# Small products of the two mixers issued in another order: level by level across four quarters of the TensorE array instead of block by block in one

## The chip, the core and the metric

The kernel runs on one core of one Trainium2 chip. The metric is the device time of one execution in microseconds (us). TensorE (PE in the profile) multiplies 128 rows by 128 columns; a product whose operands are smaller can be put on a part of the array with `tile_position=(row, column)`, and here the parts are tiles of 32x32, 128 rows x 32 columns, or 64x64. VectorE (DVE), ScalarE (ACT) and GpSimd (POOL) do the elementwise work, SyncE (SP) issues the loads of the weights.

## What is computed

One transformer layer over 256 tokens of width 2048 in float32. The normed input goes through one projection, which feeds eight heads of gated DeltaNet (GDN) and eight heads of HGRN2; the outputs of both groups go through one output projection with a residual, and a squared-ReLU feed-forward of width 8192 follows, with a residual and a last norm. Cut to what matters:

```python
def gated_delta_rule_chunked(q, k, v, beta, g):
    unit_lower = jnp.where(strict, beta[..., :, None] * kk * decay, 0.0) + jnp.eye(CHUNK, dtype=jnp.float32)
    sol = lax.linalg.triangular_solve(unit_lower, rhs, left_side=True, lower=True, unit_diagonal=True)
    ...
def hgrn2_chunked(q, k, v, log_f):
    # S_t = diag(f_t) S_{t-1} + k_t v_t^T (k_t = 1 - f_t),  o_t = S_t^T q_t
    a_diag = jnp.einsum('bhsid,bhsijd,bhsjd->bhsij', qc, d_diag, kc)
    ...
def hybrid_token_mixer(n, w_in, ...):
    proj = n @ w_in
    ...
    y = jnp.concatenate([y_a, y_b], axis=-1).astype(n.dtype)
    return y @ w_out
...
    h = h + hybrid_token_mixer(...)
    h = h + jnp.square(jax.nn.relu(rms_norm(h) @ w_ff1)) @ w_ff2
return rms_norm(h)
```

## The kernel before

**The projections.** Every weight tile is split into a high part `hi` (ACT, L117) and a rest `lo` (DVE, L118), and TensorE multiplies both: L281 (512 columns) with `hi`, L282 (256 columns) with `lo`. The result of two feature tiles is gathered in two `acc` tiles, then ACT copies (L288) and DVE adds and scales (L289, L290). The same split feeds the output projection (L655) and the feed-forward (L700, L701, L717).

**The mixers.** The kernel goes through 16 heads, and the projection of the next head stands beside the mixer of the one before it. The heads 0 to 7 are GDN; their lower triangular systems, two of 128 rows for each head, are gathered and solved together. `gdn_invert` inverts the 32x32 blocks on POOL (L413 to L427, some 60 us in a row), and `gdn_solve` (L430 to L504, called once, at the second HGRN2 head) puts the inverse together on TensorE: `Xn` holds the inverted 32x32 blocks of the 16 systems (`NB`), four of each. For the two halves `u` = 0 (rows 0 to 63) and 1 (rows 64 to 127) it multiplies the lower left block of each system with `Xn` (L454, into `pP`, the tile (0, 32) or (64, 96)), ACT negates it into `Pn` (L456), a second product goes into the other rows of `pP` (L458, the tile (32, 0) or (96, 64)), and DVE copies that into `Y` (L460). Then come `pX` (L462), two rounds of 64x64 products `pp` (L470, L475), and the products with V (L483 on). The other eight heads are HGRN2, in `hgrn_mix` (L512 to L610); they are called head 0 to 7 below. DVE prepares `E`, the keys and queries with the decays of six levels (L561, L562); TensorE then makes 40 small products into `pd`: for each of 8 blocks of 32 tokens four products of 32 columns (L575) and one of 64 (L578), on the column quarter 32q of the array, with q the number of the block modulo 4. Behind them stand three more products into `pa` (L583, L587, L589). DVE and POOL add `pd` up into `A` (L592 to L599), ACT copies `pa` to it, and `A` is multiplied with V into `poh` (L608, L609). A norm over the head follows in `finish_heads` (its products are `pm`, L393 and L394, from `shi` and `slo`, L391 and L392).

**The order.** The functions are written one after the other, but a planner takes all the instructions, with modelled durations, and writes one fixed order for each engine; each engine works its row off in that order and waits where an operand isn't there. PSUM holds four `acc` tiles, two tiles for `hgrn_mix` (`mx`) and two for the solve (`sv`), so the planner's order also depends on when these come free. All the work of the solve stands somewhere among the projections of the heads 2 to 5.

Of the kernel before, what the change touches and what calls it, by code (L numbers as in the profile page):

```python
# [16 lines left out]
T = 256  # L17
# [7 lines left out]
NL = len(LEVELS)  # L25
NM = NL + 1
# [47 lines left out]
def hybrid_block(ctx: ExitStack, tc: tile.TileContext, x, xt, w_in, w_ab, params, w_out, w_ff1, w_ff2,  # L74
                 norm_final_w, consts, out):
    nc = tc.nc
    PE, ACT, DVE, POOL, SP = nc.tensor, nc.scalar, nc.vector, nc.gpsimd, nc.sync

    def view(ap, off, dims):
        return bass.AP(ap.tensor, ap.offset + off, [list(ap.ap[0])] + [list(d) for d in dims])  # L80
# [24 lines left out]
    def mx(name):  # L105
        return psM.tile([P, 512], F32, tag="mx", name=name)
# [297 lines left out]
    NB = 2 * NH  # L404
# [25 lines left out]
    def gdn_solve(Xn):  # L430
# [13 lines left out]
        def amat(i, rows, c):  # L444
            hd, t = divmod(i, 2)
            return PA(hd)[rows, 1, t * T + c.start:t * T + c.stop]

        pP, pX = sv("pP"), sv("pX")
        Pn = Xn
        for u in range(2):  # L450
            lo_, hi_ = 64 * u, 64 * u + 32
            L_, H_ = slice(lo_, lo_ + 32), slice(hi_, hi_ + 32)
            for i in range(NB):
                PE.matmul(pP[H_, 32 * i:32 * i + 32], lhsT=amat(i, L_, H_), rhs=Xn[L_, i, :],  # L454
                          start=True, stop=True, tile_position=(lo_, hi_))
            ACT.activation(Pn[H_].rearrange("p a m -> p (a m)"), pP[H_, :], AF.Copy, scale=-1.0)  # L456
            for i in range(NB):
                PE.matmul(pP[L_, 32 * i:32 * i + 32], lhsT=Pn[H_, i, :], rhs=Yd[H_, i, :],  # L458
                          start=True, stop=True, tile_position=(hi_, lo_))
            DVE.tensor_copy(Y[L_, :, H_], pP[L_, :].rearrange("p (a m) -> p a m", m=32))  # L460
        for i in range(NB):
            PE.matmul(pX[32:64, 32 * i:32 * i + 32], lhsT=Yd[32:64, i, :], rhs=Pn[32:64, i, :],  # L462
                      start=True, stop=True, tile_position=(32, 32))
        ACT.copy(X6[32:64, :, 0:32], pX[32:64, :].rearrange("p (a m) -> p a m", m=32))
        for half in range(2):
            pp = sv("pp")
            hs = slice(8 * half, 8 * half + 8)
            for n in range(8):
                i = 8 * half + n
                PE.matmul(pp[64:128, 64 * n:64 * n + 64], lhsT=amat(i, slice(0, 64), slice(64, 128)), rhs=X6[:, i, :],  # L470
                          start=True, stop=True, tile_position=(0, 64))
            ACT.activation(P6[64:128, hs].rearrange("p a m -> p (a m)"), pp[64:128, :], AF.Copy, scale=-1.0)
            for n in range(8):
                i = 8 * half + n
                PE.matmul(pp[0:64, 64 * n:64 * n + 64], lhsT=P6[64:128, i, :], rhs=Y[64:128, i, 64:128],  # L475
                          start=True, stop=True, tile_position=(64, 0))
# [19 lines left out]
        for pair in range(NH // 2):  # L496
            po = sv("po")
            for n in range(2):
                hd, c = 2 * pair + n, n * T
# [11 lines left out]
    def hgrn_mix(hd, R):  # L511
# [6 lines left out]
        u = mp.tile([P, 4, T], F32, tag="u", name="u", bufs=UB)  # L518
# [6 lines left out]
        gx = mp.tile([P, 4, T], F32, tag="gx", name="gx")  # L525
        KQ, pb = gx[:, 0:2], gx[:, 2:4]
# [16 lines left out]
        E = mp.tile([P, NL + 2, T], F32, tag="big", name="E")  # L543
# [23 lines left out]
                          op=ALU.mult)  # L567

        pd, pa = mx("pd"), mx("pa")
        for blk in range(8):  # L570
            t, q = divmod(blk, 4)
            s = slice(32 * blk, 32 * blk + 32)
            c = t * NM * 32
            for n in range(1, NL):
                PE.matmul(pd[32 * q:32 * q + 32, c:c + 32], lhsT=E[:, n, s], rhs=E[:, n, s], start=True, stop=True,  # L575
                          tile_position=(0, 32 * q))
                c += 32
            PE.matmul(pd[32 * q:32 * q + 32, c:c + 64], lhsT=KQ[:, 0, s], rhs=view(gx, T + 32 * blk, [[T, 2], [1, 32]]),  # L578
                      start=True, stop=True, tile_position=(0, 32 * q))
        for c in range(4):  # L580
            t, q = divmod(c, 2)
            o0 = t * T + 64 * q + 32
            PE.matmul(pa[64 * q:64 * q + 32, o0:o0 + 32], lhsT=E[:, 0, 64 * c:64 * c + 32],  # L583
                      rhs=E[:, 0, 64 * c + 32:64 * c + 64], start=True, stop=True, tile_position=(0, 64 * q))
        for t in range(2):
            o0 = t * T + 64
            PE.matmul(pa[0:64, o0:o0 + 64], lhsT=E[:, NL, t * P:t * P + 64],  # L587
                      rhs=E[:, NL + 1, t * P + 64:t * P + 128], start=True, stop=True)
        PE.matmul(pa[:, P:T], lhsT=L[:, 0].rearrange("p a t -> p (a t)"), rhs=L[:, 1].rearrange("p a t -> p (a t)"),  # L589
                  start=True, stop=True)  # L590
# [24 lines left out]
    for n in range(2 * NH):  # L615
        if n + 1 < 2 * NH:
            nx = gdn_project(n + 1) if n + 1 < NH else hgrn_project(n + 1 - NH)
        if n == SOLVE_AT:
            gdn_solve(Xn)
        if n < NH:  # L620
            gdn_mix(n, *st)
        else:
            hgrn_mix(n - NH, st)
        if n == INVERT_AT:
            Xn = gdn_invert()
        st = nx
# [16 lines left out]
    for nh in range(2):  # L643
        accs = [acc_a() for _ in range(4)]
        for kp in range(8):
            w = wtile()
            SP.dma_start(w, w_out[nh * 8 + kp])
            for kk in range(2):
                k = 2 * kp + kk
                hi, lo = split(w[:, kk * 1024:(kk + 1) * 1024], 1024)  # L650
                for hf in range(2):
                    for a, ww in ((0, hi), (T, hi), (0, lo)):
                        st = yT(k, a + hf * P, a + hf * P + P)
                        for c in range(2):
                            PE.matmul(accs[2 * hf + c], lhsT=st, rhs=ww[:, c * 512:(c + 1) * 512],  # L655
                                      start=(k == 0 and a == 0 and ww is hi), stop=(k == 2 * NH - 1 and ww is lo))
# [64 lines left out]
    for f in range(NF):  # L721
# [4 lines left out]
        n = f - (NF - TAIL)  # L726
# [20 lines left out]
    for hf in range(2):  # L747
# [13 lines left out]
        s = fin[:, 2 * NP + hf:2 * NP + hf + 1]  # L761
# [61 lines left out]
```

## Times and profile before

| | us |
|---|---|
| median of three runs | 1284.4 (1284.13 to 1284.76) |
| the profiled execution, its own time | 1285.84 |
| its span (first to last instruction on the engines) | 1283.9 |
| TensorE busy in the span | 1252.5 (98%) |
| VectorE busy | 858.5 (67%) |
| ScalarE busy | 673.8 (52%) |
| GpSimd busy | 180.4 (14%) |

The time beside the span is 1.94 us. Busy time is the time in which an engine works on at least one instruction. The stages on the span's clock: the GDN heads to about 250 us, POOL's inversion from 259 to 322, the HGRN2 heads with the solve from 264 to 509, the output projection from 457 on between them, and the feed-forward from 570 to the end. The rows further down give times on the same clock.

### The profile page before, as it was taken

What the parts mean: (1) busy time and instruction counts of PE and PEld (TensorE: products, weight loads), DVE (VectorE), ACT (ScalarE), POOL (GpSimd) and SP (SyncE); (2) the same over time, 40 slices, a digit from 0 to 9 for tenths busy, and PEclk for the clock granted to TensorE, in tenths of its full rate; (3) what the DMA queues carried; (4) which work ended last, traced back from release to release, by engine and by line L of the source; (5) the groups of instructions that cost most, each with busy time, mean ns of one, the idle gap of its engine ahead of it and who ended that gap; (6) DMA issues with size and microseconds to landing.
All of it is one profiled execution on the core that took longest, in us unless ns stands there. A gap on an engine that the chain in (4) does not pass through costs nothing.

```text
span 1283.9 us, 18498 instructions
## 1 busy us (share of the span) xinstructions
PE 1252.5 (98%) x7290; PEld 1063.2 (83%) x7290; DVE 858.5 (67%) x1200; ACT 673.8 (52%) x972; POOL 180.4 (14%) x224
## 2 busy tenths in 40 slices
PE   6999999998899999999999999999999999999997
PEld 5888888877788887888888888888888888888885
DVE  8789999888867996565556555565555555555556
ACT  7567677655556874454444443444444444444453
POOL 4233433278301121000000000000000000000000
PEclk9999999998999999999999999999999999999999
DMA  7455555543423644455555555555555555555552
GB/s 289 166 160 184 174 180 192 171 140 131 149 100 131 217 151 168 154 203 191 194 173 190 196 174 189 197 175 186 197 195 190 188 191 192 194 194 197 197 200 95
DMA packets 34646, 229.65 MB, mean 179 GB/s; under 512 B 4408, under 2 KB 5184, under 8 KB 7808
## 3 DMA queue, kind: packets, MB, share of 16 engines
q1 hardware_dynamic: 32256, 225.32, 49.8%
q0 software_dynamic: 1728, 2.11, 1.3%
q8 instruction: 57, 0.93, 0.3%
q10 hardware_dynamic: 576, 1.05, 0.2%
q14 instruction: 29, 0.24, 0.1%
HBM read 225.83 MB, written 2.63 MB: 178 GB/s over the span
## 4 chain that ended last, share of the span: by engine, by line
PE 91%; DVE 3%; POOL 3%; issue 2%; DMA 1%; ACT 0%; SPq 0%; POOLq 0%; DVEq 0%; ACTq 0%
PE acc L281 15%; PE acc L717 14%; PE accb L717 13%; PE accb L700 9%; PE acc L700 9%; PE acc L282 8%; PE acc L655 7%; PE accb L701 5%; PE acc L701 5%; POOL Xt L419 1%; POOL X L421 1%; PE pd L575 1%; DVE xT L163 1%; DMA big<-in_xt_dram 1%; PE pk L363 1%
## 5 line engine op out<-in xcount | busy, mean ns | idle before, releaser
L118 DVE TENSOR_TENSOR lo<-w,hi 128x1024 fp32r<-128x1024 f32 x408 | 511.5, 1255 | 364.6 <-ACT hi L117 364.1
L117 ACT CAST hi<-w 128x1024 fp32r<-128x1024 f32 (+1 forms) x416 | 432.6, 1042 | 447.3 <-PE accb L717 177.2
L281 PE MATMUL acc<-xT,hi 128*128 128x512 f32 x1024 | 363.2, 401 | 9.6 <-ACT hi L117 8.5
L282 PE MATMUL acc<-xT,lo 128*128 128x256 f32 x1024 | 282.8, 285 | 4.8 <-DVE lo L118 4.7
L281 PEld LDWEIGHTS acc<-xT,hi 128*128 128x128 f32 x1024 | 191.0, 190 | 49.1 <-ACT hi L117 8.5
L282 PEld LDWEIGHTS acc<-xT,lo 128*128 128x128 f32 x1024 | 194.8, 191 | 12.1 <-DVE lo L118 6.2
L700 PE MATMUL acc<-hT,hi 128*128 128x512 f32 x512 | 181.3, 399 | 0.0
L700 PE MATMUL accb<-hT,hi 128*128 128x512 f32 x512 | 180.8, 398 | 0.0
L717 PE MATMUL accb<-hi,gs 128*128 128x512 f32 x496 | 170.6, 389 | 0.0
L701 PE MATMUL accb<-hT,lo 128*128 128x256 f32 x512 | 143.2, 281 | 0.0
L701 PE MATMUL acc<-hT,lo 128*128 128x256 f32 x512 | 142.8, 281 | 0.0
L717 PE MATMUL acc<-hi,gs 128*128 128x512 f32 x496 | 133.4, 389 | 0.0
L700 PEld LDWEIGHTS accb<-hT,hi 128*128 128x128 f32 x512 | 96.1, 188 | 23.9
L700 PEld LDWEIGHTS acc<-hT,hi 128*128 128x128 f32 x512 | 96.1, 188 | 23.4
L159 POOL TENSOR_TENSOR fin<-fin,cst 128x1 f32<-128x1 f32 x2 | 1.1, 566 | 777.0 <-PE accb L717 769.5
L717 PEld LDWEIGHTS acc<-hi,gs 128*128 128x128 f32 x496 | 93.0, 188 | 19.4
L717 PEld LDWEIGHTS accb<-hi,gs 128*128 128x128 f32 x496 | 93.1, 188 | 19.3
L701 PEld LDWEIGHTS acc<-hT,lo 128*128 128x128 f32 x512 | 96.5, 189 | 0.2
L701 PEld LDWEIGHTS accb<-hT,lo 128*128 128x128 f32 x512 | 96.6, 189 | 0.1
L717 PE MATMUL accb<-lo,gs 128*128 128x512 f32 x248 | 95.8, 389 | 0.0
L717 PE MATMUL acc<-lo,gs 128*128 128x512 f32 x248 | 77.2, 389 | 0.0
L717 PEld LDWEIGHTS acc<-lo,gs 128*128 128x128 f32 x248 | 46.6, 188 | 9.7
(248 smaller groups left out, 1323.6 us busy)
## 6 DMA issues: line engine op xcount, KB each, us to landing
w<-in_w_ff_dram SPq DMA_DIRECT2D x128, 1024.0 KB, 4.9
w<-in_w_in_dram SPq DMA_DIRECT2D x62, 1024.0 KB, 5.0
w<-in_w_out_dram SPq DMA_DIRECT2D x16, 1024.0 KB, 4.9
big<-in_xt_dram SPq DMA_DIRECT2D x4, 512.0 KB, 7.9
w<-in_w_in_dram SPq DMA_DIRECT2D x4, 512.0 KB, 8.1
h<-in_x_dram SPq DMA_DIRECT2D x2, 1024.0 KB, 9.2
dt<-scr_g POOLq DMA_DIRECT2D x8, 128.0 KB, 5.6
nfw<-in_norm_final_w_dram SPq DMA_DIRECT2D x1, 1024.0 KB, 4.7
```

The costliest lines, as they stand in the source:

```text
L117: ACT.copy(hi, w)
L118: eng.tensor_tensor(out=lo, in0=w, in1=hi.bitcast(F32), op=ALU.subtract)
L163: DVE.scalar_tensor_tensor(out=dst[:, k, T:2 * T], in0=pt, scalar=wcol, in1=dst[:, k, 0:T].bitcast(F32), op0=ALU.mult, op1=ALU.subtract)
L281: PE.matmul(accs[g], lhsT=hi[:, kk, g, :], rhs=xT[:, k, :], start=(k == 0), stop=False)
L282: PE.matmul(accs[g][:, T:], lhsT=lo[:, kk, g, :], rhs=xT[:, k, 0:T], start=False, stop=(k == KT - 1))
L363: PE.matmul(pk0, lhsT=R[:, 1, 0:P], rhs=qk.rearrange("p a t -> p (a t)"), start=True, stop=True)
L419: POOL.tensor_tensor(out=t3, in0=X[:, j, j + 1:].unsqueeze(2).to_broadcast([np_, nr, ncol]), in1=X[:, j, 0:ncol].unsqueeze(1).to_broadcast ...
L421: POOL.tensor_tensor(out=X[:, j + 1:, 0:ncol], in0=X[:, j + 1:, 0:ncol], in1=t3, op=ALU.subtract)
L655: PE.matmul(accs[2 * hf + c], lhsT=st, rhs=ww[:, c * 512:(c + 1) * 512], start=(k == 0 and a == 0 and ww is hi), stop=(k == 2 * NH - 1 and ...
L700: PE.matmul(accs[f], lhsT=hi[:, cs], rhs=hT[:, k, :], start=(k == 0), stop=False)
L701: PE.matmul(accs[f][:, T:], lhsT=lo[:, cs], rhs=hT[:, k, 0:T], start=False, stop=(k == KT - 1))
L717: PE.matmul(accs[hf][c], lhsT=gs[:, a + hf * P:a + hf * P + P], rhs=ww[:, cs], start=(f == 0 and a == 0 and ww is hi), stop=(f == NF - 1 a ...
```

## The change

Two groups of loops are written in another order; no product, copy or operand is added or taken away. In `gdn_solve` the two halves `u` stand inside the loop over the 16 systems, so that the products of both halves alternate; the two copies of ACT and the two of DVE follow behind each group. In `hgrn_mix` the loop over the levels stands outside and that over the 8 blocks inside, so that a product stands on another quarter than its neighbours.

```diff
 def gdn_solve(Xn):
-        for u in range(2):
-            lo_, hi_ = 64 * u, 64 * u + 32
-            L_, H_ = slice(lo_, lo_ + 32), slice(hi_, hi_ + 32)
-            for i in range(NB):
+        LH = [(64 * u, 64 * u + 32, slice(64 * u, 64 * u + 32), slice(64 * u + 32, 64 * u + 64)) for u in range(2)]
+        for i in range(NB):
+            for lo_, hi_, L_, H_ in LH:
                 PE.matmul(pP[H_, 32 * i:32 * i + 32], lhsT=amat(i, L_, H_), rhs=Xn[L_, i, :],
                           start=True, stop=True, tile_position=(lo_, hi_))
+        for lo_, hi_, L_, H_ in LH:
             ACT.activation(Pn[H_].rearrange("p a m -> p (a m)"), pP[H_, :], AF.Copy, scale=-1.0)
-            for i in range(NB):
+        for i in range(NB):
+            for lo_, hi_, L_, H_ in LH:
                 PE.matmul(pP[L_, 32 * i:32 * i + 32], lhsT=Pn[H_, i, :], rhs=Yd[H_, i, :],
                           start=True, stop=True, tile_position=(hi_, lo_))
+        for lo_, hi_, L_, H_ in LH:
             DVE.tensor_copy(Y[L_, :, H_], pP[L_, :].rearrange("p (a m) -> p a m", m=32))
...
 def hgrn_mix(hd, R):
-        for blk in range(8):
-            t, q = divmod(blk, 4)
-            s = slice(32 * blk, 32 * blk + 32)
-            c = t * NM * 32
-            for n in range(1, NL):
-                PE.matmul(pd[32 * q:32 * q + 32, c:c + 32], lhsT=E[:, n, s], rhs=E[:, n, s], start=True, stop=True,
-                          tile_position=(0, 32 * q))
-                c += 32
-            PE.matmul(pd[32 * q:32 * q + 32, c:c + 64], lhsT=KQ[:, 0, s], rhs=view(gx, T + 32 * blk, [[T, 2], [1, 32]]),
-                      start=True, stop=True, tile_position=(0, 32 * q))
+        for n in range(1, NL + 1):
+            for blk in range(8):
+                t, q = divmod(blk, 4)
+                s = slice(32 * blk, 32 * blk + 32)
+                c = t * NM * 32 + (n - 1) * 32
+                if n < NL:
+                    PE.matmul(pd[32 * q:32 * q + 32, c:c + 32], lhsT=E[:, n, s], rhs=E[:, n, s], start=True, stop=True,
+                              tile_position=(0, 32 * q))
+                else:
+                    PE.matmul(pd[32 * q:32 * q + 32, c:c + 64], lhsT=KQ[:, 0, s],
+                              rhs=view(gx, T + 32 * blk, [[T, 2], [1, 32]]),
+                              start=True, stop=True, tile_position=(0, 32 * q))
```

In the changed file some lines have other numbers: L454 is L453 there, L458 L459, L462 L464, L470 L472, L475 L477, L575 L578, L578 L581, L583 L587, L587 L591, L589 L593, L592 L596.

The planner is run anew on the changed program. The row of TensorE at the first HGRN2 head, before (the dots stand for seven more pairs of L575 and L578):

```order
L282 MATMUL acc<-xT,lo 128x256
L575 MATMUL pd<-E 32x32 x4
L578 MATMUL pd<-gx 32x64
...
L583 MATMUL pa<-E 32x32 x4
L587 MATMUL pa<-E 64x64 x2
L589 MATMUL pa<-L 128x128
```

The same place in the changed kernel:

```order
L282 MATMUL acc<-xT,lo 128x256
L578 MATMUL pd<-E 32x32 x32
L581 MATMUL pd<-gx 32x64 x8
L587 MATMUL pa<-E 32x32 x4
L591 MATMUL pa<-E 64x64 x2
L593 MATMUL pa<-L 128x128
```

The products are the same 40; the 32 short ones now stand in front of the 8 long ones, and two neighbours are never in one quarter.

TensorE at the first product of the solve, which stands inside the `pd` of head 2; before, with the half u = 0 alone (the numbers behind the names tell the tiles apart):

```order
L282 MATMUL acc_3623<-xT_100,lo_3647 128x256
L575 MATMUL pd_3544<-E_3522 32x32 x3
L454 MATMUL pP_2945<-Xn_2427,big_83 32x32 x10
L454 MATMUL pP_2945<-Xn_2427,PA1_141 32x32 x6
L575 MATMUL pd_3544<-E_3522 32x32
L578 MATMUL pd_3544<-gx_3511 32x64
```

In the changed kernel, where one of the 32 products of both halves is inside that `pd` and 31 stand behind seven products of the projection:

```order
L578 MATMUL pd_3544<-E_3522 32x32 x4
L453 MATMUL pP_2945<-Xn_2427,big_83 32x32
L578 MATMUL pd_3544<-E_3522 32x32 x28
L581 MATMUL pd_3544<-gx_3511 32x64 x8
...
L281 MATMUL acc_3623<-xT_100,hi_3646 128x512
L453 MATMUL pP_2945<-Xn_2427,big_83 32x32 x19
L453 MATMUL pP_2945<-Xn_2427,PA1_141 32x32 x12
L282 MATMUL acc_3623<-xT_100,lo_3647 128x256
```

The half u = 1, which before stood some 16 us later between two groups of L470, has moved up to the other half. The second product (L458, in the changed file L459) is one group of 32 as well, inside the group of L462 (L464), of which three stand ahead of it and 13 behind.

TensorE at the `pd` of head 5, where the norm of a pair of GDN heads (`pm_3173`) crosses it; before:

```order
L575 MATMUL pd_4481<-E_4459 32x32 x3
L393 MATMUL pm_3173<-shi_3174,ones_r_138 128x512
L575 MATMUL pd_4481<-E_4459 32x32
L578 MATMUL pd_4481<-gx_4448 32x64
L575 MATMUL pd_4481<-E_4459 32x32 x4
```

In the changed kernel:

```order
L281 MATMUL acc_4653<-xT_100,hi_4657 128x512
L578 MATMUL pd_4481<-E_4459 32x32 x11
L393 MATMUL pm_3173<-shi_3174,ones_r_138 128x512
L578 MATMUL pd_4481<-E_4459 32x32 x17
L394 MATMUL pm_3173<-slo_3175,ones_r_138 128x512
L578 MATMUL pd_4481<-E_4459 32x32 x4
L581 MATMUL pd_4481<-gx_4448 32x64 x8
```

The second half of the norm, L394, which before stood 22 products of the projection behind this `pd`, now stands inside it, and the `pd` itself stands seven products of the projection later than before. The rows of SP and POOL are the same in both kernels, and behind the last head's `pd` the rows of all engines are the same.

## Rows read from the trace of the kernel before

In the timeline the columns are the start in us, the us from the first start to the last end, the engine, line, operation, output and inputs, the size, and the number of records; TensorE works on one of these float32 products in two passes, and each pass is a record, so 40 products are 80 records.

**Rows 1.** The page: TensorE's busy time, its share of the span and its instructions; and the chain that ended last, in shares of the span.

```profile
PE 1252.5 (98%) x7290; PEld 1063.2 (83%) x7290; DVE 858.5 (67%) x1200; ACT 673.8 (52%) x972; POOL 180.4 (14%) x224
...
PE 91%; DVE 3%; POOL 3%; issue 2%; DMA 1%; ACT 0%; SPq 0%; POOLq 0%; DVEq 0%; ACTq 0%
```

**Rows 2.** The windows of five stretches: start and end, length, and for PE, PEld, DVE, ACT and POOL the busy us and the instructions, then the granted clock of TensorE, the DMA share and GB/s.

```profile
290.00:326.50 36.50, 30.36 (x230) 25.38 (x229) 30.35 (x45) 18.20 (x32) 30.57 (x43) 0.91 0.33 115
326.50:370.00 43.50, 43.04 (x517) 37.33 (x518) 38.20 (x75) 25.80 (x44) 9.17 (x13) 0.96 0.47 159
410.00:455.00 45.00, 45.00 (x413) 39.16 (x411) 43.66 (x84) 34.51 (x59) 8.26 (x10) 1.00 0.52 187
455.00:475.00 20.00, 20.00 (x181) 16.82 (x180) 18.80 (x34) 14.73 (x28) 4.80 (x6) 1.00 0.49 163
475.00:500.00 25.00, 25.00 (x196) 20.79 (x195) 20.32 (x35) 14.36 (x27) 4.78 (x6) 1.00 0.55 189
```

**Rows 3.** The timeline of TensorE in the `pd` and `pa` of head 0.

```profile
264.01 0.47 PE L575 MATMUL pd<-E 128*32 128x32 f32 x10
264.29 0.22 PE L578 MATMUL pd<-gx 128*32 128x64 f32 x1
...
264.50 0.22 PE L578 MATMUL pd<-gx 128*32 128x64 f32 x1
...
265.75 0.22 PE L583 MATMUL pa<-E 128*32 128x32 f32 x2
265.77 0.20 PE L575 MATMUL pd<-E 128*32 128x32 f32 x1
265.80 0.20 PE L583 MATMUL pa<-E 128*32 128x32 f32 x1
265.81 0.22 PE L578 MATMUL pd<-gx 128*32 128x64 f32 x1
265.81 0.25 PE L583 MATMUL pa<-E 128*32 128x32 f32 x4
265.86 0.22 PE L578 MATMUL pd<-gx 128*32 128x64 f32 x1
265.87 0.20 PE L583 MATMUL pa<-E 128*32 128x32 f32 x1
266.01 0.45 PE L587 MATMUL pa<-E 128*64 128x64 f32 x4
```

**Rows 4.** The windows of two stretches inside a `pd`, of head 0 and of head 1, columns as in rows 2.

```profile
264.25:265.65 1.40, 1.40 (x73) 1.40 (x70) 1.40 (x3) 0.00 (x0) 0.00 (x0) 1.00 0.00 0
300.60:302.00 1.40, 1.40 (x47) 1.40 (x46) 1.40 (x3) 0.00 (x0) 0.00 (x0) 0.50 0.00 0
```

**Rows 5.** The timeline of TensorE where the last products of L458 and the first of L462 meet (u = 0).

```profile
345.30 1.10 PE L458 MATMUL pP<-Yd,Xn 32*32 32x32 f32 x29
346.21 0.21 PE L462 MATMUL pX<-Xn,Yd 32*32 32x32 f32 x1
346.24 0.19 PE L458 MATMUL pP<-Yd,Xn 32*32 32x32 f32 x1
346.26 0.19 PE L462 MATMUL pX<-Xn,Yd 32*32 32x32 f32 x1
```

**Rows 6.** The timeline of TensorE at L458 of the half u = 1, and at what stands behind it.

```profile
357.89 1.19 PE L458 MATMUL pP<-Yd,Xn 32*32 32x32 f32 x32
359.01 0.38 PE L282 MATMUL acc<-xT,lo 128*128 128x256 f32 x1
```

**Rows 7.** The chain that ended last, in order of time, in front of 326.5 us: start, us, what.

```profile
322.32 0.70 POOL u L538
...
325.11 1.35 DVE lo L118
...
326.50 0.50 PE acc L282 x2
```

**Rows 8.** The sum over six windows of 10 us each from 415 to 475 us, columns as in rows 2.

```profile
sum 60.00, PE 60.00 PEld 51.62 DVE 57.60 ACT 46.36 POOL 12.74; mean PE 10.00 PEld 8.60 DVE 9.60 ACT 7.73 POOL 2.12
```

**Rows 9.** The timeline of TensorE in the `pd` of head 5, where L393 breaks it.

```profile
446.42 0.23 PE L575 MATMUL pd<-E 128*32 128x32 f32 x2
446.58 0.49 PE L393 MATMUL pm<-shi,ones_r 128*128 128x512 f32 x1
447.00 0.26 PE L575 MATMUL pd<-E 128*32 128x32 f32 x4
```

**Rows 10.** The timeline of VectorE: the `lo` tile of the weights that TensorE multiplies in front of that `pd` in the changed order, and the `slo` of the norm.

```profile
441.97 1.21 DVE L118 TENSOR_TENSOR lo<-w,hi 128x1024 fp32r<-128x1024 f32 x1
...
447.39 0.67 DVE L392 TENSOR_TENSOR slo<-fsq,shi 128x512 fp32r<-128x512 f32 x1
```

**Rows 11.** The waits of TensorE between 250 and 530 us: what waited for what, us in total, times, longest.

```profile
PE acc L282 <- DVE lo L118: 4.7, 3, 2.8
PE acc L655 <- ACT yTb L117: 2.9, 1, 2.9
```

**Rows 12.** The timeline of TensorE at the last of these waits, at the end of the mixers; from the start of the first row to that of the second stand twelve records of L655, six of them in the first row.

```profile
512.48 2.93 PE L655 MATMUL acc<-hi,yTb 128*128 128x512 f32 x6 [2.93 <-ACT yTb L117]
...
517.77 0.63 PE L669 MATMUL accb<-cst,h 128*128 128x128 f32 x2
```

**Rows 13.** The window just behind that wait, columns as in rows 2.

```profile
512.60:517.60 5.00, 5.00 (x12) 3.90 (x13) 1.59 (x4) 0.45 (x1) 0.00 (x0) 0.50 0.47 187
```

## The prediction

> **What bounds the kernel now.** I read the page first. TensorE is busy for 98% of the span, and the chain that ended last lies on it for 91% [rows 1]: a microsecond is won where TensorE's own work gets shorter and nothing else ends last there. Both edited places lie between 264 and 500 us, so I read this stretch in windows [rows 2]. From 290 to 326.5 TensorE stands idle for 6.1 of 36.5 us and POOL is busy for 30.6. The chain there runs through POOL's inversion, and at its end through POOL's `u` at 322.32, DVE's `lo` at 325.11 and TensorE at 326.50 [rows 7]. From 326.5 on TensorE is busy for 43.0 of 43.5 us, and then without a gap to 500. So the `pd` of head 0 (264 us) and of head 1 (about 300 us) lie ahead of a wait that POOL ends, while those of heads 2 to 7 and all of the solve lie where TensorE is the bound. One warning stands in the same windows: between 410 and 455 DVE is busy too, 43.7 of 45 us, and over 415 to 475 it is idle for only 2.4 of 60 us [rows 8].
>
> **What one `pd` costs now.** Head 0's runs unbroken: first record at 264.01, the last long one at 265.86, L587 at 266.01 [rows 3]. That is 2.00 us for the whole and 1.85 for 80 records, 23 ns each. Two things in these rows say how quarters work. Ten short records stand ahead of the first long one, but block 0 has only eight: two of the next block, in the next quarter, have overtaken the long ones. And at the end the products of L583 begin at 265.75 while the last block is still at work in its own quarter. So quarters do run beside each other, as far as the row of instructions lets the next one in. Inside a quarter a short record takes 31 ns: 29 of them from 345.30 to 346.21, all in one tile [rows 5]. A block alone in its quarter would need 8 x 31 ns, and for the two long records twice 63 ns (an estimate: double the columns, double the time), 0.375 us; the next block comes after 0.21 (264.29 to 264.50). Before, less than two quarters are at work at a time.
>
> **The 40 products in the new order.** Four quarters with two blocks each need 2 x 0.375 = 0.75 us, if nothing else limits them. What else could is the pace at which TensorE starts records. The nearest rows are 265.75 to 265.87: ten records for three quarters in 0.12 us, 12 ns each. Four quarters would want 0.75/80 = 9 ns. I take the pace that the rows show: 80 x 12 ns = 0.96 us, then 0.10 for the eight records of L583, which now find all quarters equally late, then 0.15 to L587 as now. That makes 1.21 instead of 2.00, **0.79 us less for each head**; with 0.75 (and L583 at 31 ns for four records in a quarter, 0.125) it is 0.98, and the lower bound is nothing, if the pace stays at 23 ns.
>
> Against a fixed pace of 23 ns speaks head 1, which meets the same row of instructions at half the granted clock: 47 records in 1.40 us, where head 0 has 73 at the full clock [rows 4]. A pace that the issue sets would not follow the array's clock. It does not double either (29.8 against 19.2 ns), so a fixed part is in it, 19.2 - (29.8 - 19.2) = 8.6 ns at most: no more than the 9 that are wanted. The Trainium skill says otherwise ("TensorE: Matmul & The Clock Gate", section "Wait — 56ns, not 53.3ns?"): two matmuls never start less than about 25 ns apart, however small they are. By that rule, an estimate, 80 records take 2.0 us in any order and the heads gain nothing; the 19 ns of rows 4 and the 12 ns of rows 3 do not agree with it.
>
> Six heads on the path: 6 x 0.79 = **4.7 us**. Heads 0 and 1 I count at nothing, because POOL's inversion covers them; without that cover they would be worth 1.6 more.
>
> **The solve.** A group of 16 products of one half is 32 records in one tile: L458 of u = 1 from 357.89 to 359.01, 1.12 us with the change of shape around it [rows 6]. Four such groups are made, two of L454 and two of L458. Side by side, two halves need the time of one: 64 records at 12 ns are 0.77, less than 1.12, so the tile sets the time. Two groups fall away, 2 x 1.12 = **2.2 us**. That two small tiles do alternate is seen at 346.21 to 346.26, where L458 and L462 start 20 to 30 ns apart, each within the time of a record of the other [rows 5]. Those two write to different PSUM tiles, `pP` and `pX`, and start from the same rows of the array; in the change both halves write to `pP` from different rows. Nothing before shows that. If it is not possible, the gain is zero at worst (one after the other, as now).
>
> **What is given back.** With a shorter `pd` in heads 4 to 6, TensorE wants to be 2.4 us earlier over the stretch in which DVE has 2.4 us of idle time [rows 8]. If DVE can use all of it, nothing is lost; if half, 1.2. I take 0.8. In head 5 the planner has moved L394 into the `pd`, which is now broken twice. One break shows at 446.42 to 447.00 [rows 9]: L393 holds the row for 0.42 us, and about 0.1 of that and the 0.16 ahead of it are the change of shape. I take 0.3 for the second break. ACT's and DVE's copies of the solve now follow a group of both halves, so that the first is about as late as the second used to be in its own group; the solve is spread over 100 us of projections, which cover it.
>
> **Sum.** 4.7 + 2.2 - 0.8 - 0.3 = 5.8 us. The profiled execution took 1285.84, 1.44 above the median of the runs; so 1280.0 for it, and **1278.6** against the median. Its own range: 1276.4 (0.98 for each head, nothing given back but the break) to 1280.
>
> **Rivals.** A measurement of this kernel can tell about 0.2%, 2.6 us.
>
> A: the pace of about 22 ns is TensorE's own, and the order of quarters doesn't matter to it. The heads gain nothing; 64 records of the solve at 22 ns take 1.4 instead of 2.24, twice 0.85 = 1.7; less the break: 1283.0, no change that can be told. For it: no stretch of before holds 12 ns for longer than ten records, and those may have stood ready in their quarters. Against it: rows 4. The Trainium skill's 25 ns end here too.
>
> B: the two halves in one PSUM tile take turns. The solve gains nothing: 4.7 - 1.1 = 3.6, 1280.8. The Trainium skill warns of just that ("TensorEngine Tiling (Array Packing)", section "Gotcha 1: PSUM Pressure"): tiles in different rows cannot access the same PSUM bank at the same time. No run here shows it yet.
>
> C: DVE becomes the bound from 415 to 475, and the 2.4 us of heads 4 to 6 are lost whole: 4.7 + 2.2 - 2.4 - 0.3 = 4.2, 1280.2. TensorE's waits for DVE's `lo` would show it.
>
> D: a new wait with a slower clock behind it. The place is L394 in the `pd` of head 5, which needs `slo`. In the order of before `slo` ends at 448.06 [rows 10], 4.9 us behind the `lo` of 441.97 that ends at 443.18; in the changed row of DVE the operations between them are 0.7 us less, so 447.4. TensorE gets to L394 seven products of the projection later than the old start of this `pd`, 445.4 + 1.2, and behind L393 and 56 short records: about 447.8. So 0.4 us are to spare as long as both engines keep in step, and TensorE has won up to 4.6 us (the solve and heads 2 to 4) before it gets there, which DVE must match out of its idle time. All projection products queue behind L394. Price: the last wait of the mixers was 2.9 us [rows 11, 12], and the clock was 0.50 in the 5 us behind it [rows 13], where 5.3 us of L655 took twice their time: 2.6 more, 5.5 together. So 1284.1, level with before; a second one of the kind would make it slower.
>
> E, the other side: alternation undoes the overlap. If TensorE lets a record start in another quarter only when the one before it is through, each costs what it costs alone: 64 x 31 + 16 x 63 ns = 3.0 us instead of 1.85, +1.17 for each of six heads, 7.0, and the break; the solve stays as it is: 1291.7. It decides from 28 ns per record on (0.43 us more for a head, 2.6 in six). For it: before, the overlap comes only at the change of block. Against it: 12 ns across three quarters [rows 3].
>
> F: all goes well, and a stretch at the lower clock (0.96 in the mean from 326.5 to 370, so 0.04 x 2 x 43.5 = 3.5 us at half, worth 1.7) falls away besides: 5.9 + 2.2 + 1.7 - 0.3 = 9.5, 1274.9.
>
> **Chances.** Forecast 0.47, A 0.11, B 0.12, C 0.10, D 0.10 (0.03 of it slower, with a second wait), E 0.06, F 0.04. Faster by over 0.2%: forecast, B, C and F, 0.73. The same: A and most of D, 0.18. Slower: E and the rest of D, 0.09. The range from 1274.5 to 1284.3 leaves out E, the double wait of D and a little at either end.
>
> **What the changed profile would show.** Right: the `pd` of an unbroken head, first record to L587, takes about 1.2 us (0.9 to 1.3), at 9 to 12 ns per record; 64 records of the first product of the solve take about 1.1 to 1.2 us, with starts alternating; TensorE stays busy from 326.5 to 500 us, and the feed-forward begins some 6 us earlier. Wrong: a `pd` of 2.0 (A) or 3 us (E); 64 records of the solve in 2.2 (B); waits for `lo` between 415 and 475 (C); a wait of L394 at `slo` with a stretch at half clock behind it (D). Heads 0 and 1 should be shorter as well, and TensorE's wait for POOL ahead of 326.5 longer by as much.

## Result

The changed kernel takes 1276.83 us (median of four runs, 1276.28 to 1277.50) against 1284.58 beside it (1284.13 to 1287.41): 7.7 us less by the medians, and 8.3 by the ratio, 0.9935 (interval 0.9918 to 0.9952), which takes in all runs and not the middle ones alone. Two more groups of runs gave 0.9935 (0.9922 to 0.9948) and 0.9941 (0.9927 to 0.9956) for the same kernel. The prediction said 1278.6, 5.8 us less, with a range of 1274.5 to 1284.3. The direction and the mechanism were right; the gain was a third larger than the sum.

### The profile after

The page after: TensorE's busy time, share and instructions, and the chain by engine.

```profile
PE 1243.4 (97%) x7290; PEld 1054.2 (83%) x7290; DVE 857.5 (67%) x1200; ACT 674.2 (53%) x972; POOL 178.7 (14%) x224
...
PE 91%; DVE 3%; POOL 3%; issue 2%; DMA 1%; ACT 0%; SPq 0%; POOLq 0%; DVEq 0%; ACTq 0%
```

TensorE's busy time is 9.1 us less than in [rows 1]; the chain's shares are the same. Its work became shorter, and nothing took its place as the bound.

TensorE at head 0, after, to be held against [rows 3]:

```profile
263.82 0.73 PE L578 MATMUL pd<-E 128*32 128x32 f32 x62
264.37 0.23 PE L581 MATMUL pd<-gx 128*32 128x64 f32 x1
...
264.40 0.41 PE L581 MATMUL pd<-gx 128*32 128x64 f32 x14
264.60 0.32 PE L587 MATMUL pa<-E 128*32 128x32 f32 x8
264.85 0.45 PE L591 MATMUL pa<-E 128*64 128x64 f32 x4
```

From 263.82 to 264.37 start 62 short records, 9 ns apart. The first product of 64 columns of `pa` (now L591) comes 1.03 us after the first record; before it was 2.00. The whole of `pd` and the short products of `pa` take the time that one quarter needs for its share: 0.75 + 0.125 + 0.15 = 1.02 us was the other end of the prediction's estimate.

The second product of the solve after (L459 is L458 before), both halves in `pP`, with L464 (L462 before) around it:

```profile
344.53 0.22 PE L459 MATMUL pP<-Yd,Xn 32*32 32x32 f32 x2
...
344.62 1.01 PE L459 MATMUL pP<-Yd,Xn 32*32 32x32 f32 x53
...
345.47 0.22 PE L459 MATMUL pP<-Yd,Xn 32*32 32x32 f32 x3
...
345.57 0.60 PE L464 MATMUL pX<-Xn,Yd 32*32 32x32 f32 x14
```

53 records take 0.85 us (344.62 to 345.47), 16 ns each. In [rows 5] a record of one half alone took 31 ns. Both halves write the same PSUM tile from different rows of the array, and run fully side by side.

The windows of `pd` between 326 and 500 us (heads 2 to 7) and of `pP` between 326 and 362: busy us (and instructions) of PE, PEld and the readers, then clock, DMA share, GB/s. Before:

```profile
326.00:500.00 174.00, 13.55 (x480) 11.97 (x480) 6.63 (x12) 0.99 0.46 159
...
326.00:362.00 36.00, 4.77 (x128) 4.33 (x128) 1.36 (x2) 1.18 (x2) 0.95 0.48 161
```

After:

```profile
326.00:500.00 174.00, 6.95 (x480) 5.42 (x480) 6.63 (x12) 0.99 0.47 165
...
326.00:362.00 36.00, 2.83 (x128) 2.38 (x128) 1.36 (x2) 1.19 (x2) 0.95 0.48 162
```

The `pd` of six heads is 6.60 us shorter in busy time, `pP` 1.94. Windows without a filter, of before and after, in the columns of [rows 2], show what lies beside it:

```profile
326.50:410.00 83.50, 83.04 (x803) 73.21 (x804) 64.34 (x118) 50.93 (x88) 12.99 (x18) 0.98 0.39 134
410.00:475.00 65.00, 65.00 (x591) 55.98 (x590) 62.45 (x118) 49.23 (x85) 13.05 (x16) 1.00 0.51 180
```

```profile
290.00:326.50 36.50, 30.44 (x232) 25.69 (x231) 30.89 (x45) 18.20 (x32) 30.58 (x43) 0.87 0.33 115
326.50:410.00 83.50, 83.22 (x832) 73.17 (x831) 70.99 (x131) 56.43 (x95) 11.99 (x18) 0.98 0.42 146
410.00:475.00 65.00, 65.00 (x593) 54.86 (x593) 60.69 (x114) 49.06 (x91) 14.70 (x17) 1.00 0.52 183
```

Up to 326.5 us TensorE is as busy as before; POOL sets the pace there. Behind that it is as full as before; DVE has done 6.7 us more by 410 us, and 1.8 us less is left for 410 to 475, the stretch in which the prediction feared that DVE would give some of the gain back. TensorE's waits between 326.5 and 500 us:

```profile
PE acc L282 <- DVE lo L118: 1.3, 1, 1.3
PE pP L453 <- issue: 0.3, 1, 0.3
```

The first of these is the wait for POOL's stage, which ends at 326.13. There is no wait for DVE or ACT behind it. The last wait of the mixers ends at 504.27, 178.14 us later:

```profile
504.27 1.22 PE L659 MATMUL acc<-hi,yTb 128*128 128x512 f32 x2 [2.93 <-ACT yTb L117]
```

Before, that stretch went from 326.50 to 512.48 [rows 7, 12], 185.98 us. Of the 8.3 us between the two spans (1283.9 and 1275.6), 7.84 lie in this stretch and 0.4 ahead of it; from there to the end both kernels take 771.3 to 771.4 us.

### The profile page after: what moved, and what is told of

It reads as the page before. It is cut to its first block, busy times and chain, and to the rows that moved or that the text cites. A ratio compares the mean times of both kernels' runs of the same rounds, so it can differ in the third digit from the quotient of the medians.

```text
span 1275.6 us, 18490 instructions
## 1 busy us (share of the span) xinstructions
PE 1243.4 (97%) x7290; PEld 1054.2 (83%) x7290; DVE 857.5 (67%) x1200; ACT 674.2 (53%) x972; POOL 178.7 (14%) x224
## 4 chain that ended last, share of the span: by engine, by line
PE 91%; DVE 3%; POOL 3%; issue 2%; DMA 1%; ACT 0%; SPq 0%; POOLq 0%; DVEq 0%; ACTq 0%
PE acc L281 15%; PE acc L721 14%; PE accb L721 13%; PE accb L704 9%; PE acc L704 9%; PE acc L282 8%; PE acc L659 7%; PE accb L705 5%; PE acc L705 5%; POOL Xt L419 1%; POOL X L421 1%; DVE xT L163 1%; DMA big<-in_xt_dram 1%; PE pk L363 1%; DVE E L548 0%
## 5 line engine op out<-in xcount | busy, mean ns | idle before, releaser
L281 PE MATMUL acc<-xT,hi 128*128 128x512 f32 x1024 | 363.7, 401 | 10.0 <-ACT hi L117 8.3
L281 PEld LDWEIGHTS acc<-xT,hi 128*128 128x128 f32 x1024 | 192.1, 191 | 50.1 <-ACT hi L117 8.3
L721 PEld LDWEIGHTS accb<-lo,gs 128*128 128x128 f32 x248 | 46.6, 188 | 9.7
```

The costliest lines, as they stand in the source:

```text
L281: PE.matmul(accs[g], lhsT=hi[:, kk, g, :], rhs=xT[:, k, :], start=(k == 0), stop=False)
L721: PE.matmul(accs[hf][c], lhsT=gs[:, a + hf * P:a + hf * P + P], rhs=ww[:, cs], start=(f == 0 and a == 0 and ww is hi), stop=(f == NF - 1 a ...
```

## Experiments

All ratios are to the kernel before on the same chip, and the gains in microseconds are worked out from them.

**One: `pd` alone.** The second part of the change, with the solve as before.

```diff
-        for blk in range(8):
+        for n in range(1, NL + 1):
...
-            for n in range(1, NL):
+            for blk in range(8):
```

> Only the products into pd stand level by level; the solve is as before. Sum of parts: an unbroken pd takes 1.03 us from its first record to the first 64-column product of pa, as in the changed kernel, against 2.00 before; six heads on the path (2 to 7) give 5.8 us, so about 1278.7 against 1284.5, ratio 0.9955. Rival, the planner's new order is what gained: pd is as short, but the total lies more than 1.5 us from 1278.7, on either side.

Measured: 1282.11 us, ratio 0.9982 (0.9970 to 0.9993), 2.3 us by the ratio instead of 5.8. The `pd` of heads 0, 5, 6 and 7 is as short as in the changed kernel (0.77 us from first to last start). The time went elsewhere; TensorE's waits from 326.8 to 500 us:

```profile
PE pa L585 <- issue: 1.4, 1, 1.4
...
PE acc L657 <- ACT hi L117: 0.7, 1, 0.7
PE acc L657 <- DVE lo L118: 0.6, 1, 0.6
PE pm L394 <- DVE slo L392: 0.5, 1, 0.5
```

(The row left out is the end of POOL's stage.) These are 3.2 us of waits, where the kernel before has 0.5 and the changed one 0.3: 1.4 behind the `pd` of head 2, put down to issue, and 1.8 at the beginning of the output projection for DVE and ACT (L657 at 459.93 and 461.51, and L394, which stands between its products). DVE itself had waited there, at 456.3, 1.9 us for ACT's part of a norm of the GDN heads. The solve has come hardly earlier: the first product of `po` starts at 391.3 us, before at 392.4, in the changed kernel at 383.7; the last one at 436.8, 438.8 and 432.8. So TensorE won its time, and in this trace met rival C of the prediction where the norms behind the solve come late. The theory "the parts add up" is wrong for the time, though right for TensorE's work.

**Two: the solve alone.**

```diff
-        for u in range(2):
...
+        for i in range(NB):
+            for lo_, hi_, L_, H_ in LH:
```

> Only the two products of the solve alternate their halves; pd is as before. Sum of parts: the time of TensorE in pP falls from 4.4 to 2.5 us and nothing else moves, so about 1282.6, ratio 0.9985. Rival, the planner's new order: gain of nothing, or of more than 3 us. Rival, both halves in one PSUM tile take turns: pP stays at 4.4 us.

Measured: 1283.42 us, ratio 0.9988 (0.9980 to 0.9997), 1.5 us where 1.9 were expected; the window of `pP`:

```profile
326.00:362.00 36.00, 2.64 (x128) 2.30 (x128) 1.36 (x2) 1.18 (x2) 0.91 0.41 135
```

2.13 us less than before. From the wait for POOL to the last wait of the mixers this trace takes 185.22 us (327.40 to 512.62), only 0.76 less than before: the granted clock is 0.50 for 6.8 us of it (between 326.2 and 333.2), where the trace of before has 3.4 (between 327.4 and 331.0), which costs 1.7 us more. The two ratios together make 3.8 us, both edits in one kernel 8.3. What the parts lack is open after these two.

**Three: heads 0 and 1 as before.**

```diff
+        if hd < 2:
+            for blk in range(8):
+                ... (block by block, as before)
+        else:
             for n in range(1, NL + 1):
```

> The changed kernel, but heads 0 and 1 of HGRN2 make pd block by block as before. If POOL's inversion covers both heads, the time is that of the changed kernel, 1276.8, though pd of heads 0 and 1 takes 1 and 2 us longer, and the waits of TensorE ahead of 326 us are shorter by as much. If heads 0 and 1 count, 1278.8 to 1279.8.

Measured: 1276.37 us, ratio 0.9935 (0.9922 to 0.9948), beside 0.9935 for the changed kernel itself in the same group. POOL covers the two heads wholly; the gain lies in heads 2 to 7.

**Four: the changed kernel again,** no edit.

> The changed kernel once more, beside the three above: 1276.8, ratio 0.994, as the measure for them.

Measured: 1276.06 us, ratio 0.9935 (0.9922 to 0.9948).

**Five: the new order of statements, but no alternation in the solve.** Both products of L454 first, then both copies, then both products of L458; each half's 16 products in one group.

```diff
-        for i in range(NB):
-            for lo_, hi_, L_, H_ in LH:
+        for lo_, hi_, L_, H_ in LH:
+            for i in range(NB):
```

> The changed kernel, with the solve's statements in the changed order (both products of L454, then both copies, then both products of L458), but each half's 16 products in one group, so that neighbours stand in one tile again. If the change had two effects in the solve, 1.9 us on the array and an earlier end of the solve that the planner makes of the new order of statements, then pP takes 4.4 us again, the last product of po still ends near 434 us instead of 437 to 439, TensorE doesn't wait near 460 us, and the time is 1.9 us above that of the changed kernel: ratio about 0.995. If the earlier end of the solve comes from the shorter products, the time falls back to that of the kernel with the change of pd alone, ratio 0.998, with waits near 460 us.

Measured: 1281.40 us, ratio 0.9969 (0.9958 to 0.9981), a wide spread (1278.38 to 1284.48). The window of `pP` and TensorE's waits from 328 to 500 us:

```profile
326.00:362.00 36.00, 4.50 (x128) 4.16 (x128) 1.36 (x2) 1.18 (x2) 1.00 0.43 147
```

```profile
PE acc L282 <- DVE lo L118: 0.5, 1, 0.5
```

(The one row is a wait at 331 us.) `pP` takes 4.50 us again, 1.67 more than in the changed kernel, and yet the first product of `po` starts at 385.7 and the last at 434.9; there is no wait near 460 us. With `pd` alone they start at 391.3 and 436.8; the solve alone, with the order of before in `pd`, has its first `po` at 387.7, its last at 438.1. So the earlier beginning of `po` comes from the order of the statements (the planner no longer spreads the two halves), not from the shorter products; that the last one comes earlier takes the shorter `pd` besides. In this trace, the stretch from 327.50 to the last wait of the mixers, at 506.48, takes 178.98 us, 0.8 more than in the changed kernel, which had 3 us at half clock in it, where this one has none. Against the trace of experiment four, the changed kernel without a stretch at half clock (326.63 to 504.32, 177.69 us), it is 1.3 more. The median lies higher than that accounts for; experiment nine is on that.

**Six: two neighbours in one quarter.**

```diff
-            for blk in range(8):
+            for blk in (0, 4, 1, 5, 2, 6, 3, 7):
```

> The changed kernel with the blocks of a level in the order 0, 4, 1, 5, 2, 6, 3, 7: two products stand in one quarter, then two in the next. If each quarter has a short queue of its own (three records deep, by the overtaking seen before), the four records of a visit fit in it and the pd of an unbroken head still takes 0.8 to 0.9 us from its first record to the first of pa: ratio as the changed kernel's, 0.9935 to 0.9945. If only neighbours in different quarters overlap, two quarters are at work at a time, pd takes about 1.5 us and six heads give back 4.3 us: ratio 0.997.

**Seven: two quarters at a time.**

```diff
-        for n in range(1, NL + 1):
-            for blk in range(8):
+        for n, g in [(n, g) for g in (0, 2) for n in range(1, NL + 1)]:
+            for blk in (g, g + 1, g + 4, g + 5):
```

> The changed kernel with all products of quarters 0 and 1 first, alternating, then all of 2 and 3, alternating. Neighbours still stand on different quarters. If the time is that of the fullest quarter at 31 ns per short record, each of the two phases takes 0.75 us, less some 0.1 where they meet: pd 1.4 us, 0.6 more than in the changed kernel for each of six heads, 3.7 us in all, ratio 0.9965. If a change of quarter between neighbours is what counts, or the issue sets the 10 ns, pd stays at 0.8 us and the ratio at 0.9935.

**Eight: one quarter at a time.**

```diff
-        for n in range(1, NL + 1):
-            for blk in range(8):
+        for n, g in [(n, g) for g in range(4) for n in range(1, NL + 1)]:
+            for blk in (g, g + 4):
```

> The changed kernel with all products of quarter 0 first, then of 1, 2, 3: ten products in a row in one quarter. Queue of three records per quarter: the next quarter's first record starts after 17 of 20, so pd takes 3 x 17 x 0.0375 + 0.75 = 2.7 us against 1.85 before and 0.78 after, 11 us more than the changed kernel for six heads, ratio about 1.002. If the pace is the same in any order, pd takes 0.8 to 1.9 us and the kernel is no slower than before.

Measured, with the first records of head 0, the last one of `pd` (L581) and L591 in the timeline. Six, pairs: 1277.70 us, ratio 0.9937 (0.9924 to 0.9950).

```profile
264.03 0.76 PE L578 MATMUL pd<-E 128*32 128x32 f32 x58
...
264.95 0.22 PE L581 MATMUL pd<-gx 128*32 128x64 f32 x1
...
265.19 0.45 PE L591 MATMUL pa<-E 128*64 128x64 f32 x4
```

Seven, two quarters: 1278.75 us, ratio 0.9948 (0.9936 to 0.9959).

```profile
264.18 0.70 PE L578 MATMUL pd<-E 128*32 128x32 f32 x32
...
265.43 0.22 PE L581 MATMUL pd<-gx 128*32 128x64 f32 x1
...
265.70 0.45 PE L591 MATMUL pa<-E 128*64 128x64 f32 x4
```

Eight, one quarter: 1285.73 us, ratio 1.0001 (0.9991 to 1.0011).

```profile
265.23 0.69 PE L578 MATMUL pd<-E 128*32 128x32 f32 x16
265.75 0.22 PE L581 MATMUL pd<-gx 128*32 128x64 f32 x1
265.76 0.25 PE L578 MATMUL pd<-E 128*32 128x32 f32 x2
...
267.52 0.22 PE L581 MATMUL pd<-gx 128*32 128x64 f32 x1
267.68 0.45 PE L591 MATMUL pa<-E 128*64 128x64 f32 x4
```

From the first to the last start, `pd` takes 0.92, 1.25 and 2.29 us, against 0.77 in the changed kernel and 1.85 before. The same 80 records in five orders: the time follows how many quarters are kept at work. Pairs cost almost nothing, so it is not the neighbour that counts: each quarter holds a few records waiting while the row goes on to the next. With one quarter at a time the next one begins behind 17 of the 20 records, at 265.76, as the three waiting records of the expectation have it. Two quarters came out 0.15 below the expected 1.4, one quarter 0.4 below 2.7. I had spread the long records evenly over each quarter's 20; they stand last there, so that more of the time lies behind the point where the next quarter is let in, 0.53 us after the first record (3 x 0.53 + 0.75 = 2.34). Six heads at 2.29 instead of 0.77 make 9.1 us; the ratio says 8.5. Six heads at 1.25 make 2.9 us, a ratio of 0.9957; 0.9948 was measured, with 0.9957 inside its interval.

**Nine: the grouped kernel of experiment five again.**

> The kernel with the changed order of statements but each half in one group, once more: its trace had it 1.3 us behind the changed kernel up to the output projection, its runs 4.4 us. If a wait that comes in some executions only is the difference, this trace or the spread of the runs shows it, among the waits put down to issue above all (code arriving late at the small products near 338 us); the median then lies again 3 us or more above the changed kernel beside it. If the first medians were a matter of that chip, the kernel is 1.9 us above the changed kernel here.

Measured: 1285.03 us, ratio 0.9989 (0.9973 to 1.0004). Its runs fall at two times: nine of 12 between 1284.6 and 1285.5, three between 1278.0 and 1278.5. The trace is one of the first kind. TensorE's waits from 328 to 500 us (the second row joins POOL's wait and one at 331 us), the timeline around the largest, the instruction queue of the DMA engines from 337.0 to 337.5 us (packets, MB, share), and two windows behind it:

```profile
PE pa L587 <- issue: 1.9, 1, 1.9
PE acc L282 <- DVE lo L118: 1.9, 2, 1.4
```

```profile
337.31 0.29 PE L587 MATMUL pa<-E 128*32 128x32 f32 x6
339.50 0.32 PE L587 MATMUL pa<-E 128*32 128x32 f32 x2 [1.89 <-issue]
```

```profile
q8 instruction: 1, 0.02, 11.6%
```

```profile
339.40:346.00 6.60, 6.50 (x50) 5.66 (x51) 3.93 (x9) 3.47 (x6) 0.77 (x2) 0.50 0.44 161
353.20:356.00 2.80, 2.80 (x11) 2.46 (x10) 1.35 (x4) 0.79 (x2) 0.00 (x0) 0.50 0.68 287
```

Behind the `pd` of head 2, with 16 products of the solve in it, TensorE stands still for 1.89 us with nothing to wait for in the profile but issue. A block of instructions (16 KB) started to arrive at 337.23, and TensorE goes on some 2.3 us later. In the trace of experiment five, of the same kernel, a block arrives between 332 and 333 us, none between 335 and 338, and there is no stall. Behind the stall the granted clock is 0.50 in both windows shown, where experiment five has 1.00; between 339.3 and 356.4 two such stretches make 10.2 us at half clock, worth 5.1. The stretch from 327.62 to 513.04 takes 185.42 us, 6.4 more than in experiment five. In the kernel with `pd` alone the same place has 1.4 us, in the kernel before 0.5, in the changed kernel 0.3 or nothing (0.6 with heads 0 and 1 as before).

Counted through the traces, the place is the same in every kernel: in front of the 1998th or 1999th of TensorE's 7290 records, whether that is a product of `pa` (before, with `pd` alone, here) or of `pP` (the others). In seven traces (before, the changed kernel, experiments one, three, eight, nine and eleven) TensorE stands still there and goes on 2.2 to 2.4 us after a block started to arrive (336.25 and 338.67 before, 337.91 and 340.10 in experiment three). In the other seven it gets to that record 2.4 to 8.9 us behind the start of the block and doesn't stand still. So what decides is how early TensorE gets there. That the wait is for code is read from this place and these times; no run moved the block by itself. Why the block sometimes comes 5 us earlier stays open. That the other executions near 1285 us have the stall too is not shown, since only one of them was traced.

**Ten: the changed kernel, third time,** no edit.

> The changed kernel beside the three others of this call: ratio 0.9935, and a pd of 0.77 us from first to last start in heads 0, 6 and 7.

Measured: 1277.23 us (1274.95 to 1278.90), ratio 0.9941 (0.9927 to 0.9956); no stall, although the block of instructions starts at 336.3: TensorE gets to the record of experiment nine only at 338.75, 2.4 us later.

**Eleven: more products beside others.** `pX` goes into the loop of L459 as a third tile, the short products of `pa` between the levels of `pd`.

```diff
                 PE.matmul(pP[L_, 32 * i:32 * i + 32], lhsT=Pn[H_, i, :], rhs=Yd[H_, i, :],
                           start=True, stop=True, tile_position=(hi_, lo_))
+            PE.matmul(pX[32:64, 32 * i:32 * i + 32], lhsT=Yd[32:64, i, :], rhs=Pn[32:64, i, :],
+                      start=True, stop=True, tile_position=(32, 32))
```

> The changed kernel, with the four short products of pa between the levels of pd, and the 16 products of pX (tile (32, 32)) as a third one beside the two halves of the second product of the solve. By the time of the fullest quarter: pX's 1.0 us goes, and pa costs its quarters 0.13 us inside pd in place of 0.25 behind it, 0.1 for each of six heads: 1.6 us less than the changed kernel, ratio 0.9923. Rival: the planner's order or DVE takes it back, ratio 0.9935 or above.

Measured: 1276.95 us, ratio 0.9939 (0.9926 to 0.9953); not to be told from the changed kernel beside it. Counted from the start of each record to that of the next, `pX` holds TensorE for 0.32 us instead of 0.97; in the six heads `pa` holds it for 0.66 less and `pd` for 0.79 more (its first to last start is now 0.87 us), because the four short products stand in quarters that were full.

**Twelve: the 64x64 products alternated as well.**

```diff
-        for half in range(2):
+        for step in range(3):
...
+                if step > 0: ...  tile_position=(64, 0)
```

> The kernel with pa and pX moved, and besides the 64x64 products: the second product of the first half of the systems (tile (64, 0)) alternates with the first product of the second half (tile (0, 64)). Eight of 32 products then run beside eight others: the time of TensorE in pp falls from 4.0 to 3.0 us, the sum is 2.6 us less than the changed kernel, ratio 0.9915. Rival: the planner's order or DVE takes it back, ratio 0.9935 or above.

Measured: 1276.25 us, ratio 0.9933 (0.9919 to 0.9947), level with the changed kernel. The planner did not follow: it put all products of L473 in one group and all of L477 in another, six us later, and the window of `pp` is what it was (4.15 us busy in both).

```profile
350.00:362.00 12.00, 4.15 (x64) 3.88 (x64) 0.68 (x1) 1.08 (x2) 1.00 0.36 133
```

## Why the prediction was right, and where its size was off

**The bound, and heads 0 and 1.** Right. TensorE's work from 326 us on was the time; the two heads ahead of it count for nothing (experiment three).

**The 40 products.** The mechanism was right: quarters run side by side up to the time of the fullest (experiments six to eight; A and E fall). The 31 ns for a record in one quarter were read in a tile of 32x32; in the quarters themselves it is 32 (16 records in 0.52 us, experiment eight). The size was off: I took a pace of 12 ns from ten records of the old order, and the chip kept 9. The gain is 0.97 us for an unbroken head, not 0.79; six heads make 5.8 instead of 4.7, which is 1.1 of the 1.9 us that the sum lacked. The ten records that I read do not show the pace: seven of them and the one behind them are the eight of L583, four for each of two quarters; at 31 ns a quarter needs 0.125 us for its four, so the time of those quarters can have set the 0.12 us by itself. The other end of that estimate, 0.98, was the right one, and head 1 at half clock [rows 4] had said that no more than 8.6 ns are fixed. The Trainium skill ("TensorE: Matmul & The Clock Gate", section "Wait — 56ns, not 53.3ns?") puts 25 ns at least between two starts; 62 starts in 0.55 us do not agree with it.

**The solve.** 2.2 forecast, 1.94 less busy. Two halves in one PSUM tile do run side by side, at 16 ns per record: B falls. The Trainium skill warns ("TensorEngine Tiling (Array Packing)", section "Gotcha 1: PSUM Pressure") that tiles in different rows cannot access the same PSUM bank at the same time; this trace does not agree with it, for tiles that write to different partitions, as here.

**What is given back.** The 0.8 us for DVE were not given back in the changed kernel, and were (1.8 us) in the trace of the kernel with `pd` alone. Beside the pace, the step that failed is that I costed the new order of statements at nothing: it lets the planner begin the products `po` earlier (the first at 383.7 instead of 392.4, and at 385.7 with the order of statements but without the alternation), and DVE's share of them moves out of the crowded stretch: from 326.5 to 410 us DVE is busy for 64.3 us before, 65.7 with `pd` alone, 70.2 in experiment five and 71.0 in the changed kernel. The second break of head 5 came as forecast:

```profile
440.34 0.39 PE L578 MATMUL pd<-E 128*32 128x32 f32 x22
440.66 0.49 PE L393 MATMUL pm<-shi,ones_r 128*128 128x512 f32 x1
441.09 0.50 PE L578 MATMUL pd<-E 128*32 128x32 f32 x34
441.52 0.50 PE L394 MATMUL pm<-slo,ones_r 128*128 128x512 f32 x1
441.95 0.27 PE L578 MATMUL pd<-E 128*32 128x32 f32 x8
...
442.49 0.45 PE L591 MATMUL pa<-E 128*64 128x64 f32 x4
```

L393 and L394 each hold the row for 0.43 us, and L591 comes 2.15 us after the first record instead of 1.03: 0.56 for each break, 0.3 more than a product of 512 columns costs among its like (0.23 from start to start for L281 ahead of L459). L394 did not have to wait: `slo` was through at 440.73, 0.8 us ahead of it.

**The sum.** 4.7 + 2.2 - 0.8 - 0.3 becomes 5.8 + 1.9 - 0 - 0.3 = 7.4; the trace has 7.84 between the two marks. The heads were put 1.1 too low and DVE's share cost 0.8 that did not come; the solve, 0.3 too high, hid a little of that. Two sums of the prediction are slightly off, without consequence: its own range begins at 1276.6, not 1276.4 (5.9 + 2.2 - 0.3 = 7.8), and the extra time of a head in E is 1.14, not 1.17.

**Rival F** had the heads right, at 0.98, and not the clock: no stretch at the lower clock fell away (3.4 us at half clock from 327.4 on before, 3.3 from 326.1 on after), so the gain between the two traces is not the clock's.

**Rival D** had the right price at another place: not L394 at `slo`, but a stall for issue with a slower clock behind it, 6.4 us in experiment nine. It decides between kernels whose products on TensorE differ by less than 2 us. The changed kernel all but escapes it: seven products of the projection stand between the `pd` of head 2 and 62 of the 64 records of the solve's first product, and TensorE gets to the record where the stall stands about when the wait is over. Of the 4.5 us by which the two parts alone fall short of both together, the trace of experiment one shows 2.7 (3.2 us of waits, where the kernel before had 0.5 in the same place); the trace of experiment two lost 1.7 to the clock, but its execution took 1284.69 us, 1.3 more than the median of its kernel. The rest, about what the intervals of the ratios leave open, is not settled.

## What to carry to other kernels

Give each quarter of the array its share before you come back to it, but two in a row do no harm: what counts is that no quarter runs dry. Read the pace that an order could reach from the time of one quarter, not from the places where the old order happened to change quarters. A planner turns a new order of statements into a new place for everything behind it, so test the parts of an edit one by one, and look at two traces before you believe the difference.

## What the runs showed of the hardware

TensorE starts float32 records of 32 columns 9 ns apart when four quarters take turns (62 in 0.55 us), and 31 ns apart in one tile alone [rows 5]. A quarter keeps a few records waiting while the row goes on: four in a row in one quarter cost 0.15 us over 80 records, and with 20 in a row the time tripled (0.77 to 2.29 us). Two tiles of different rows and columns run side by side into different partitions of one PSUM tile, at 16 ns per record. And code seems to be a thing that is waited for: at one and the same place in its row TensorE stood still, for up to 1.9 us and in seven of 14 traces, until 2.2 to 2.4 us after a block of instructions had started to arrive; behind the stall of 1.9 us it then worked 10 us at half the clock, behind that of 1.4 us it did not.
